# Identity products behind the sums and the transposes of each norm, and another pace for the first layer's modulation

## The chip, the cores and the metric

The kernel runs on one core of a Trainium2 chip. The metric is the device time of one execution in microseconds (us), the median of several executions. The profile is taken of one execution of its own.

## What is computed

Two layers of a transformer trunk over 256 tokens of 2048 values, in float32. Each layer has a mixer and a gated feed-forward part (ffn). Ahead of each stands an RMS norm, scaled and shifted by values that a condition vector `c` gives, and the result is added through a gate of the same kind:

```python
c_act = jax.nn.silu(c)
for i in range(DEPTH):
    mod = c_act @ ada_w[i] + ada_b[i]
    sh1, sc1, g1, sh2, sc2, g2 = [m[:, None, :] for m in jnp.split(mod, 6, axis=-1)]
    h = rms_norm(x, norm_mix_g[i]) * (1.0 + sc1) + sh1
    y = even_mixer(h, ...) if i % 2 == 0 else odd_mixer(h, ...)
    x = x + g1 * y
    h = rms_norm(x, norm_ffn_g[i]) * (1.0 + sc2) + sh2
    x = x + g2 * conv_ffn(h, ffn_w_up[i], ffn_conv_w[i], ffn_conv_b[i], ffn_w_down[i])
return rms_norm(x, final_g)
```

`ada_w[i]` has 2048 rows and 6 x 2048 columns, so the modulation alone reads 192 MiB for both layers.

## The kernel before

**Tiling.** The residual stream `xT` stays in SBUF transposed, as 16 blocks of 128 values by 256 tokens. Weights come in pieces of 128 x 1024 values (512 KB, `make_piece`, L147 to L167) through a ring of six buffers (tile `w`), one piece ahead of use. A piece of the first projection is used as it is, in float32. Every later piece is split: ScalarE rounds it to `hi` (L159), VectorE takes the rest `lo` (L161), and TensorE multiplies three times.

**The modulation.** It has 192 rows (here a row is a 128 x 2048 tile of 1 MB that gives one block of one of the six vectors of a layer). `ada_step` (L109 to L124) starts the transfer of one row on SyncE's queue (SP, L118) into a ring of two buffers (tile `ada`), and VectorE multiplies it by `c_act` and sums it (L120); for a scale one small product more follows (L124). Rows go in the order of use: scale and shift of the first mixer block by block, its gate, scale and shift of the ffn, the ffn's gate, and so on. When a row is asked for is set by a pace: `pacing(rate, ...)` (L131) sets how many rows each weight piece brings, and `beat` (L134) adds the rate at every piece and calls `ada_step` when a whole row is due. Apart from that, `modulate` (L314) asks for a row at once where it needs one. In the opening (L412 to L433) each block of the first norm asks for its two rows so, 32 in all. Then the pace is 0.83 (L434) until the end of `mixer_out`. Between the two stand 26 pieces of the first projection and 32 of the output projection, 58 in all. The first inner norm needs 48 rows beyond the opening's: the gate of the mixer and scale and shift of the ffn. From there the pace is 0.31, later 0.2 and 0.15.

**The norms.** There are five: `in` (opening), then `o0_` ahead of the first ffn, `dn` of layer 0, `o1_`, and `dn` of layer 1 (the last; behind it only the output is scaled and written). `norm_rstd` (L295 to L309) sums the squares over the 128 values of a block on TensorE with a column of ones into tile `nps` (products of one column), VectorE turns the sums into the mean (`v`, L304), GpSimd takes the power -0.5 (`y`, L292), and TensorE transposes it to all partitions (`r`, L308). Then `modulate` makes each block with VectorE and ScalarE.

**What sets the order.** The tile framework's scheduler orders each engine's instructions when the program is built; each engine then works through its list in order. So instructions of the code can change places on an engine, and a changed number moves others. SyncE issues its transfers in order too: behind a row that waits for its buffer the pieces wait.

**The end of the first mixer.** `mixer_out` (L351) multiplies the output projection in two halves of the rows; in each, pairs of blocks are multiplied (`dense2`) and added to `xT` by VectorE (`residual`, L349). In the second half the pairs of blocks also go into the norm's sum (`norm_add`), and the last two blocks are done one by one (`last_blocks`).

Of the kernel before, what the change touches and what calls it, by code (L numbers as in the profile page):

```python
# [60 lines left out]
def trunk(ctx, tc, x, c, params, consts, rel_bias, onehot, w_ada, w_ev, w_o0, w_f0, w_od, w_o1, w_f1, out):  # L61
    nc = tc.nc
# [8 lines left out]
    def bank(tag, name):  # L71
        return ps.tile([P, 512], F32, tag=tag, bufs=BANKS[tag], name=name)
# [19 lines left out]
    def cn(name):  # L92
        a, b = C_AT[name]
        return con[:, a:b]

    ident, exch = cn("ident"), cn("exch")
# [34 lines left out]
    def pacing(rate, hold=0, behind=True):  # L131
        pace.update(rate=rate, hold=hold, behind=behind)
# [106 lines left out]
    def halved(acc):  # L239
        return acc.rearrange("p (j s) -> p j s", j=2)  # L240
# [48 lines left out]
    def rsqrt(v, name):  # L289

        y = work.tile([P, 2], F32, tag="rs_y", bufs=2, name=f"y_{name}")
        nc.gpsimd.tensor_tensor(y, v, mhalf, op=ALU.pow)  # L292
        return y

    def norm_rstd(st):  # L295

        t = bank("t", f"nps_{st['name']}")
        parts = [st["sum"][:, j] for j in range(2)] + st["last"]
        for i, part in enumerate(parts):
            for q in range(2):  # L300
                nc.tensor.matmul(t[:, q:q + 1], part[:, q * P:(q + 1) * P], ones, start=i == 0 and q == 0,
                                 stop=i == len(parts) - 1, skip_group_check=True)
        v = work.tile([P, 2], F32, tag="rs_v", bufs=2, name=f"v_{st['name']}")
        nc.vector.tensor_scalar(v, t[:, :2], 1.0 / D, EPS, op0=ALU.mult, op1=ALU.add)  # L304
        y = rsqrt(v, st["name"])
        r = bank("t", f"r_{st['name']}")
        for q in range(2):
            nc.tensor.transpose(r[:, q * P:(q + 1) * P], y[:, q:q + 1].to_broadcast([P, P]), ident)  # L308
        return r[:, :S]  # L309

    def modulated(name):
# [74 lines left out]
    def even_mixer():  # L386
        with ExitStack() as es:
# [33 lines left out]
            nst = {"name": "in", "sum": total[:, 0:2], "last": [total[:, 2], total[:, 3]]}  # L421
            r = pool.tile([P, 384], F32, tag="z", bufs=2, name="r_in")[:, :S]
            nc.scalar.activation(r, norm_rstd(nst), AF.Copy)
            early = [(token_steps32, bank("acc", "c_lat")), (token_steps32, bank("acc", "va"))]
            early += [(pair_steps32, bank(tag, f"pair{i}")) for i, tag in enumerate(("acc", "s", "s", "o", "t", "t"))]
# [5 lines left out]
                    else:  # L431
                        pair_steps32(acc, hT, [k], 0, DB - 1)
            c_acc, va_acc, p0, p1, p2, p3, p4, p5 = [halved(acc) for _, acc in early]  # L433
            pacing(0.83, 0, False)  # L434
            nc.sync.dma_start(par[:, P_EARLY:], params[:, P_EARLY:])
            nc.sync.dma_start(con[:, P:], consts[:, P:C_W])

# [382 lines left out]


    nst = even_mixer()
    pacing(0.31, 0)
    nst = ffn(norm_rstd(nst), 0)
    pacing(0.2, 5)
    nst = odd_mixer(norm_rstd(nst))
    pacing(0.15, 5)
    nst = ffn(norm_rstd(nst), 1)
# [132 lines left out]
```

## Time and profile before

| | us |
|---|---|
| median of 3 runs | 2358.72 (2341.0 to 2361.32) |
| profiled execution | 2362.08 |
| its span | 2360.3 |

The mean granted clock of TensorE is 0.99 in the profiled execution. A profile counts an engine as busy while an instruction of its runs. "Idle before <-releaser" is the time that an engine stood still ahead of an instruction, and what ended that. The granted clock is a share of TensorE's full clock of 2.4 GHz; 0.50 is its lower level, 1.2 GHz. A float32 product shows as two records.

### The profile page before, as it was taken

What the parts mean: (1) busy time and instruction counts of PE and PEld (TensorE: products, weight loads), DVE (VectorE), ACT (ScalarE), POOL (GpSimd) and SP (SyncE); (2) the same over time, 40 slices, a digit from 0 to 9 for tenths busy, and PEclk for the clock granted to TensorE, in tenths of its full rate; (3) what the DMA queues carried; (4) which work ended last, traced back from release to release, by engine and by line L of the source; (5) the groups of instructions that cost most, each with busy time, mean ns of one, the idle gap of its engine ahead of it and who ended that gap; (6) DMA issues with size and microseconds to landing.
All of it is one profiled execution on the core that took longest, in us unless ns stands there. A gap on an engine that the chain in (4) does not pass through costs nothing.

```text
span 2360.3 us, 44197 instructions
## 1 busy us (share of the span) xinstructions
PE 2283.0 (97%) x18340; PEld 2240.1 (95%) x18340; DVE 1738.4 (74%) x2390; ACT 1092.9 (46%) x1553; POOL 12.0 (1%) x26
## 2 busy tenths in 40 slices
PE   5889999899999999999999999999999999999998
PEld 4768899899999999999999999999999999999998
DVE  4557689998887888888887676878766656656655
ACT  1013354455553554454456655645555445445434
POOL 1000000000000000000000000000000000000000
PEclk9999999999999999999999999999999999999999
DMA  8998988788888888888867777676766666666663
GB/s 313 344 335 326 331 305 312 286 313 302 303 298 299 304 300 304 300 304 301 304 226 240 237 238 239 226 260 204 231 188 187 187 186 185 188 187 187 188 187 118
DMA packets 141929, 606.03 MB, mean 257 GB/s; under 512 B 15584, under 2 KB 20256, under 8 KB 117024
## 3 DMA queue, kind: packets, MB, share of 16 engines
q1 hardware_dynamic: 136656, 597.67, 74.8%
q10 hardware_dynamic: 5072, 5.54, 0.8%
q8 instruction: 143, 2.34, 0.4%
q14 instruction: 58, 0.48, 0.1%
HBM read 601.00 MB, written 2.15 MB: 256 GB/s over the span
## 4 chain that ended last, share of the span: by engine, by line
PE 53%; issue 32%; DMA 7%; DVE 6%; ACT 1%; POOL 0%; ACTq 0%; DVEq 0%; POOLq 0%; SPq 0%
PE up L215 7%; PE up L213 7%; PE up L214 7%; DMA ada<-in_w_ada_dram 6%; DVE ada L120 4%; PE dn L213 3%; PE dn L214 3%; PE dn L215 3%; PE o L213 2%; PE o L215 2%; PE o L214 2%; PE cq L213 1%; PE ck L213 1%; PE cq L214 1%; PE ck L214 1%
## 5 line engine op out<-in xcount | busy, mean ns | idle before, releaser
L159 ACT ACTIVATE hi<-w 128x1024 fp32r<-128x1024 f32 x688 | 728.6, 1059 | 890.7 <-PE up L214 389.6
L161 DVE TENSOR_TENSOR lo<-w,hi 128x1024 fp32r<-128x1024 f32 x688 | 840.5, 1223 | 402.5 <-ACT hi L159 399.9
L213 PE MATMUL up<-hT_f,hi 128*128 128x256 f32 x2816 | 789.5, 281 | 2.8 <-ACT hT_f L323 2.2
L215 PE MATMUL up<-hT_f,lo 128*128 128x256 f32 x2816 | 788.6, 280 | 0.2 <-DVE lo L161 0.2
L214 PE MATMUL up<-hT_f,hi 128*128 128x256 f32 x2816 | 787.4, 280 | 0.0
L213 PEld LDWEIGHTS up<-hT_f,hi 128*128 128x128 f32 x2816 | 529.5, 188 | 3.7 <-ACT hT_f L323 2.9
L215 PEld LDWEIGHTS up<-hT_f,lo 128*128 128x128 f32 x2816 | 530.6, 189 | 0.5 <-DVE lo L161 0.4
L214 PEld LDWEIGHTS up<-hT_f,hi 128*128 128x128 f32 x2816 | 529.9, 188 | 0.0
L120 DVE CUSTOM_DVE_ANT_0 ada<-ada,c_act,par 128x2048 f32<-128x2048 f32 x192 | 450.5, 2346 | 78.8 <-DMA ada<-in_w_ada_dram 78.7
L214 PE MATMUL dn<-gT,hi 128*128 128x256 f32 x1364 | 383.8, 281 | 0.0
L215 PE MATMUL dn<-gT,lo 128*128 128x256 f32 x1364 | 383.8, 281 | 0.0
L213 PE MATMUL dn<-gT,hi 128*128 128x256 f32 x1364 | 383.8, 281 | 0.0
L215 PEld LDWEIGHTS dn<-gT,lo 128*128 128x128 f32 x1364 | 262.1, 192 | 0.0
L213 PEld LDWEIGHTS dn<-gT,hi 128*128 128x128 f32 x1364 | 256.1, 188 | 0.0
L214 PEld LDWEIGHTS dn<-gT,hi 128*128 128x128 f32 x1364 | 256.1, 188 | 0.0
L228 PE MATMUL pair<-hT_m,w 128*128 128x256 f32 x384 | 89.1, 390 | 0.0
L228 PEld LDWEIGHTS pair<-hT_m,w 128*128 128x128 f32 x384 | 76.6, 199 | 11.6
L349 DVE SCALAR_TENSOR_TENSOR xT<-dn,mod,xT 128x256 f32<-128x256 f32 x128 | 56.4, 478 | 25.4 <-PE dn L215 20.2
L228 PE MATMUL q<-hT_m,w 128*128 128x256 f32 x320 | 73.7, 382 | 0.0
L213 PE MATMUL cq<-hT_m,hi 128*128 128x256 f32 x256 | 72.2, 282 | 1.1 <-ACT hT_m L323 1.1
L214 PE MATMUL cq<-hT_m,hi 128*128 128x256 f32 x256 | 72.1, 282 | 0.0
L213 PE MATMUL ck<-hT_m,hi 128*128 128x256 f32 x256 | 72.0, 281 | 0.0
(260 smaller groups left out, 3071.3 us busy)
## 6 DMA issues: line engine op xcount, KB each, us to landing
w<-in_w_f_dram SPq DMA_DIRECT2D x528, 512.0 KB, 4.4
ada<-in_w_ada_dram SPq DMA_DIRECT2D x192, 1024.0 KB, 6.5
w<-in_w_od_dram SPq DMA_DIRECT2D x96, 512.0 KB, 4.4
w<-in_w_o_dram SPq DMA_DIRECT2D x64, 512.0 KB, 5.3
w<-in_w_ev_dram SPq DMA_DIRECT2D x58, 512.0 KB, 7.9
bias<-bias_rows ACTq DMA_DIRECT2D x16, 256.0 KB, 6.2
xT<-in_x_dram SPq DMA_DIRECT2D x4, 512.0 KB, 7.6
c_act<-in_c_dram SPq DMA_DIRECT2D x1, 1024.0 KB, 4.9
```

Source lines behind the costliest of these rows:

```text
L120: nc.vector.tensor_tensor_reduce(w, w, c_act, scale=1.0, scalar=pr("ada_b")[:, s * DB + b:s * DB + b + 1], op0=ALU.mult, op1=ALU.add, accu ...
L159: nc.scalar.activation(hi, raw, AF.Copy)
L161: sub = nc.vector.tensor_tensor(lo, raw, hi.bitcast(F32), op=ALU.subtract)
L213: nc.tensor.matmul(o, hi[:, js], xh, start=k == first and j == 0, stop=False, skip_group_check=True)
L214: nc.tensor.matmul(o, hi[:, js], xl, start=False, stop=False, skip_group_check=True)
L215: nc.tensor.matmul(o, lo[:, js], xh, start=False, stop=k == last, skip_group_check=True)
L228: nc.tensor.matmul(acc[:, j * S:(j + 1) * S], w[:, j * P:(j + 1) * P], xs[:, k], start=k == first and j == 0, stop=k == last, skip_group_c ...
L349: nc.vector.scalar_tensor_tensor(xT[:, b], acc, g, xT[:, b], op0=ALU.mult, op1=ALU.add)
```

## The change

A new helper `busy` multiplies the identity by itself n times, 128 x 128, into columns 128 to 255 of the tile that holds the norm's sums in its first two columns. Nobody reads these columns. `norm_rstd` calls it with 4 behind the products of the sums and with 6 behind the transposes, in all five norms. And the pace of the first layer's modulation behind the opening is 0.95 rows for each piece instead of 0.83.

```diff
--- before.py
+++ after.py
@@ -292,6 +292,11 @@
         nc.gpsimd.tensor_tensor(y, v, mhalf, op=ALU.pow)
         return y
 
+    def busy(spare, n):
+
+        for i in range(n):
+            nc.tensor.matmul(spare, ident, ident, start=False, stop=i == n - 1, skip_group_check=True)
+
     def norm_rstd(st):
 
         t = bank("t", f"nps_{st['name']}")
@@ -300,12 +305,14 @@
             for q in range(2):
                 nc.tensor.matmul(t[:, q:q + 1], part[:, q * P:(q + 1) * P], ones, start=i == 0 and q == 0,
                                  stop=i == len(parts) - 1, skip_group_check=True)
+        busy(t[:, 128:256], 4)
         v = work.tile([P, 2], F32, tag="rs_v", bufs=2, name=f"v_{st['name']}")
         nc.vector.tensor_scalar(v, t[:, :2], 1.0 / D, EPS, op0=ALU.mult, op1=ALU.add)
         y = rsqrt(v, st["name"])
         r = bank("t", f"r_{st['name']}")
         for q in range(2):
             nc.tensor.transpose(r[:, q * P:(q + 1) * P], y[:, q:q + 1].to_broadcast([P, P]), ident)
+        busy(t[:, 128:256], 6)
         return r[:, :S]
 
     def modulated(name):
@@ -431,7 +438,7 @@
                     else:
                         pair_steps32(acc, hT, [k], 0, DB - 1)
             c_acc, va_acc, p0, p1, p2, p3, p4, p5 = [halved(acc) for _, acc in early]
-            pacing(0.83, 0, False)
+            pacing(0.95, 0, False)
             nc.sync.dma_start(par[:, P_EARLY:], params[:, P_EARLY:])
             nc.sync.dma_start(con[:, P:], consts[:, P:C_W])
```

The lists of three engines change as follows. Line numbers of the changed kernel are larger by 5 behind the helper, by 6 behind the first call and by 7 behind the second. Each of the changed lists has the same operations under other buffer numbers.

VectorE at the norm of the opening; `v_in` is the read of the sums, `ada` with the line under it is one row's reduction, `a` its scale, `xn_m` the first block. Before:

```order
L420 TENSOR_TENSOR sq_in_110<-sq_in_110,sq_in_118 128x1024
L304 TENSOR_SCALAR v_in<-nps_in 128x2
L120 ISA ada_147,mod<-ada_147,c_act,par 128x2048
L120 ISA mod 128x1
L124 SCALAR_TENSOR_TENSOR a_93<-mod,par 128x1
L319 SCALAR_TENSOR_TENSOR xn_m_154<-r_in,a_93,xT 128x256
L120 ISA ada_151,mod<-ada_151,c_act,par 128x2048
```

After the change:

```order
L427 TENSOR_TENSOR sq_in_110<-sq_in_110,sq_in_118 128x1024
L120 ISA ada_157,mod<-ada_157,c_act,par 128x2048
L120 ISA mod 128x1
L310 TENSOR_SCALAR v_in<-nps_in 128x2
L124 SCALAR_TENSOR_TENSOR a_93<-mod,par 128x1
L120 ISA ada_161,mod<-ada_161,c_act,par 128x2048
L120 ISA mod 128x1
L326 SCALAR_TENSOR_TENSOR xn_m_164<-r_in,a_93,xT 128x256
L120 ISA ada_189,mod<-ada_189,c_act,par 128x2048
```

The first row's reduction stands ahead of the read of the sums, and the second ahead of the first block.

VectorE ahead of the first inner norm; `xT<-o_1_14` and `xT<-o_1_15` are the last two residuals of the mixer, `v_o` the norm's read, `xn_f` its first block. Before:

```order
L120 ISA mod 128x1
L286 TENSOR_TENSOR nsum_o__2755<-nsum_o__2755,sq_o_12_3112 128x512
L124 SCALAR_TENSOR_TENSOR a_95<-mod,par 128x1
L349 SCALAR_TENSOR_TENSOR xT<-o_1_14_3115,mod,xT 128x256
L161 TENSOR_TENSOR lo_3158<-w_3154,hi_3156 128x1024
L120 ISA ada_3160,mod<-ada_3160,c_act,par 128x2048
L120 ISA mod 128x1
L349 SCALAR_TENSOR_TENSOR xT<-o_1_15_3153,mod,xT 128x256
L161 TENSOR_TENSOR lo_3250<-w_3246,hi_3248 128x1024
L304 TENSOR_SCALAR v_o__3200<-nps_o__3191 128x2
L161 TENSOR_TENSOR lo_3280<-w_3276,hi_3278 128x1024
L319 SCALAR_TENSOR_TENSOR xn_f_3214<-r_o__3204,a_95,xT 128x256
```

After the change:

```order
L356 SCALAR_TENSOR_TENSOR xT<-o_1_14_3147,mod,xT 128x256
L120 ISA ada_3115,mod<-ada_3115,c_act,par 128x2048
L120 ISA mod 128x1
L161 TENSOR_TENSOR lo_3152<-w_3148,hi_3150 128x1024
L120 ISA ada_3154,mod<-ada_3154,c_act,par 128x2048
L120 ISA mod 128x1
L356 SCALAR_TENSOR_TENSOR xT<-o_1_15_3184,mod,xT 128x256
L161 TENSOR_TENSOR lo_3189<-w_3185,hi_3187 128x1024
L310 TENSOR_SCALAR v_o__3235<-nps_o__3222 128x2
L120 ISA ada_3191,mod<-ada_3191,c_act,par 128x2048
L120 ISA mod 128x1
L326 SCALAR_TENSOR_TENSOR xn_f_3255<-r_o__3239,a_95,xT 128x256
```

Ahead of the last residual stand two rows with one split between them instead of one row, and directly behind the norm's read stands a row where a split stood. Over a longer stretch, from the second residual of pair 4 of the second half (`o_1_4`) to the norm's read, VectorE's list has 6 rows before and 10 now; from the start of the program to that read it has 80 before and 86 now. The 192nd row ends 64 splits earlier.

TensorE at the same norm; `nps_o` are its sums, `r_o` the transposes, `up` the first products of the ffn. Before:

```order
L192 MATMUL o_1_15_3153<-oT_o__1706,hi_3118 128x256
L193 MATMUL o_1_15_3153<-oT_o__1706,lo_3120 128x256
L301 MATMUL nps_o__3191<-ones,nsum_o__2755 128x1 x4
L301 MATMUL nps_o__3191<-ones,sql_o_14_3151 128x1 x2
L301 MATMUL nps_o__3191<-ones,sql_o_15_3188 128x1 x2
L308 MATMUL r_o__3204<-con,y_o__3202 128x128 x2
L213 MATMUL up_0_3211<-hT_f_3210,hi_3156 128x256
L213 MATMUL up_1_3212<-hT_f_3210,hi_3248 128x256
```

After the change:

```order
L192 MATMUL o_1_15_3184<-oT_o__1726,hi_3150 128x256
L193 MATMUL o_1_15_3184<-oT_o__1726,lo_3152 128x256
L306 MATMUL nps_o__3222<-ones,sql_o_15_3219 128x1 x2
L298 MATMUL nps_o__3222<-con 128x128 x5
L314 MATMUL r_o__3239<-con,y_o__3237 128x128 x2
L298 MATMUL nps_o__3222<-con 128x128 x5
L213 MATMUL up_0_3252<-hT_f_3251,hi_3187 128x256
L213 MATMUL up_1_3253<-hT_f_3251,hi_3289 128x256
```

Of the sums only those of block 15 (`sql_o_15`) still stand directly ahead of the read; those of the pairs and of block 14 have moved ahead of the 24 products of block 15. Of the ten identity products (L298) five stand ahead of the transposes and five behind them. The read of the sums (`v_o`) waits for the fourth of the first five, the fifth waits for that read.

## Rows read from the trace of the kernel before

**Rows 1.** part 1 of the page: busy us of each engine (share of the span), instructions.

```profile
PE 2283.0 (97%) x18340; PEld 2240.1 (95%) x18340; DVE 1738.4 (74%) x2390; ACT 1092.9 (46%) x1553; POOL 12.0 (1%) x26
```

**Rows 2.** stretches: us, engines' busy us (instructions), granted clock, DMA share, GB/s.

```profile
30.00:170.00 140.00, 118.00 (x480) 97.86 (x480) 79.26 (x90) 7.42 (x15) 0.00 (x0) 0.94 0.92 338
170.00:330.00 160.00, 155.44 (x895) 139.39 (x896) 113.70 (x285) 70.07 (x203) 0.73 (x1) 1.00 0.90 328
330.00:398.00 68.00, 67.88 (x569) 66.89 (x569) 62.88 (x120) 34.79 (x78) 0.00 (x0) 1.00 0.85 302
398.00:444.00 46.00, 39.62 (x324) 38.65 (x323) 44.60 (x59) 19.44 (x23) 0.00 (x0) 0.97 0.89 331
```

**Rows 3.** chain of waits from 405 to 445 us: shares by line, one piece.

```profile
by line: DVE ada L120 34.1%; DMA ada<-in_w_ada_dram 16.0%; DVE lo L161 15.4%; DVE xT L349 9.9%; DVE nsum_o__2755 L286 6.4%; issue 4.4%; POOL y_o__3202 L292 3.8%; PE nps_o__3191 L301 2.6%; PE o L215 2.4%; PE o L213 2.4%; PE o L214 2.3%; ACT 
...
428.73 6.41 DMA ada<-in_w_ada_dram
```

**Rows 4.** VectorE's timeline: start, us, engine, line, operation, count, [idle before <-releaser].

```profile
409.97 0.87 DVE L349 SCALAR_TENSOR_TENSOR xT<-o,mod,xT 128x256 f32<-128x256 f32 x2
...
435.16 2.35 DVE L120 CUSTOM_DVE_ANT_0 ada<-ada,c_act,par 128x2048 f32<-128x2048 f32 x1 [0.46 <-DMA ada<-in_w_ada_dram]
...
439.63 2.35 DVE L120 CUSTOM_DVE_ANT_0 ada<-ada,c_act,par 128x2048 f32<-128x2048 f32 x1
...
441.90 0.48 DVE L349 SCALAR_TENSOR_TENSOR xT<-o,mod,xT 128x256 f32<-128x256 f32 x1
...
443.94 0.16 DVE L304 TENSOR_SCALAR v_o__3200<-nps_o__3191 128x2 f32<-128x2 f32 x1 [0.42 <-PE nps_o__3191 L301]
```

**Rows 5.** TensorE's timeline at that norm, same columns.

```profile
442.89 1.01 PE L301 MATMUL nps_o__3191<-ones,sql_o 128*128 128x1 f32 x4 [3.15 <-ACT sql_o L275]
...
447.66 1.01 PE L213 MATMUL up<-hT_f,hi 128*128 128x256 f32 x3 [1.12 <-ACT hT_f L323]
```

**Rows 6.** busy time and granted clock by stretch, columns as in Rows 2.

```profile
448.00:451.00 3.00, 3.00 (x15) 3.00 (x15) 3.00 (x9) 1.71 (x5) 0.00 (x0) 0.50 0.98 412
1199.00:1200.00 1.00, 0.20 (x2) 0.12 (x2) 0.56 (x2) 0.00 (x0) 0.35 (x1) 0.68 0.74 295
1202.00:1206.00 4.00, 3.79 (x18) 3.80 (x18) 4.00 (x11) 2.26 (x6) 0.00 (x0) 0.50 0.12 46
```

**Rows 7.** timeline of all engines in the opening.

```profile
22.84 0.16 DVE L304 TENSOR_SCALAR v_in<-nps_in 128x2 f32<-128x2 f32 x1 [3.67 <-PE nps_in L301]
...
25.29 4.83 SPq L118 DMA_DIRECT2D ada<-in_w_ada_dram  x2
...
27.41 2.35 DVE L120 CUSTOM_DVE_ANT_0 ada<-ada,c_act,par 128x2048 f32<-128x2048 f32 x1
```

**Rows 8.** busy time of the opening's norm, columns as in Rows 2.

```profile
22.00:26.00 4.00, 0.93 (x5) 0.85 (x6) 2.59 (x4) 0.00 (x0) 2.74 (x1) 1.00 0.00 0
```

**Rows 9.** GpSimd's power (L292): count, ns min/median/max, first and last start.

```profile
L292 POOL TENSOR_TENSOR y_dn<-v_dn,mhalf x2: 688/692/696, 1199.6 to 2349.1; 128x2 f32<-128x2 f32 x2
L292 POOL TENSOR_TENSOR y_in<-v_in,mhalf x1: 2739/2739/2739, 23.1 to 23.1; 128x2 f32<-128x2 f32 x1
...
L292 POOL TENSOR_TENSOR y_o__3202<-v_o__3200,mhalf x1: 1544/1544/1544, 444.3 to 444.3; 128x2 f32<-128x2 f32 x1
```

**Rows 10.** TensorE's timeline, 0 to 60 us.

```profile
19.22 3.58 PE L301 MATMUL nps_in<-ones,sq_in 128*128 128x1 f32 x16 [10.76 <-DVE sq_in L420]
...
41.58 5.34 PE L228 MATMUL pair<-hT_m,w 128*128 128x256 f32 x24
46.76 1.03 PE L221 MATMUL c_lat<-w,hT_m 128*128 128x256 f32 x4
```

**Rows 11.** timeline of all engines at the dn norm of layer 0.

```profile
1198.60 0.61 PE L301 MATMUL nps_dn<-ones,sql_dn 128*128 128x1 f32 x4 [0.15 <-ACT sql_dn L275]
1199.41 0.15 DVE L304 TENSOR_SCALAR v_dn<-nps_dn 128x2 f32<-128x2 f32 x1
```

**Rows 12.** modulation rows (tile ada) from 300 to 444 us.

```profile
DMA to landing us min/median/max: 4.8/6.6/8.6
```

## The prediction

> **What bounds the kernel now.** I read the page first: TensorE's rows fill 97% of the span [rows 1]. So only the places where it waits can change the end. The busy time by stage shows where they are [rows 2]. From 170 to 398 us TensorE is full or nearly so. From 398 to 444 us it is busy 39.6 us of 46 and VectorE 44.6 of 46: there VectorE sets the pace. Next the chain of waits for the end of that stretch: VectorE's reductions of modulation rows (L120) are 34.1% of the chain from 405 to 445 us, and the transfer of a row another 16.0% [rows 3]. The reader is to see in the longest piece that a row's weights were issued at 428.73 us and landed 6.41 us later, with VectorE waiting. VectorE's timeline shows what is late: the last residual before the norm stands behind a row of 2.35 us and ends only after 442 us [rows 4]. TensorE waited 3.15 us for the square made from it, and 1.12 us more for the first modulated block [rows 5].
>
> The clock of that norm is 0.50 behind it (448 to 451 us: 15 products in 3 us, the lower level, 1.2 GHz) [rows 6]. The full stretch before, at clock 1.00 (2.4 GHz), ran 569 products in 67.9 us, 0.119 each [rows 2]. At the norm after the first layer's ffn (dn) the clock falls within the microsecond from 1199 (0.68, so at about 1199.4) and is 0.50 to 1206 us; 18 products take 3.79 us there [rows 6], 0.21 each. So the lower level costs 18 x (0.21 - 0.119) = 1.7 us a norm. The opening, 30 to 170 us, is ruled by the modulation rows' transfers (DMA share 0.92, clock 0.94 [rows 2]).
>
> **The change, part by part.** *A: the opening.* The identity products put off the norm's read of the sums, and the build therefore sets the first row's reduction ahead of it. VectorE was idle 3.67 us before 22.84 us [rows 7], so the reduction now runs from about 19.2 to 21.5 us. It frees the row's buffer then instead of at 25.3 us, when SP issued the third row [rows 7]. The DMA engines moved nothing from 22 to 26 us [rows 8], so they are free to take it. The second row's reduction can run behind the norm's read. That read comes 1.8 us later (below): 24.6 us, reduction to 27.0 instead of 29.7 us (27.41 + 2.35 [rows 7]). After that each block's odd row waits for a buffer freed by the odd row before it, so the shift travels through the opening: 2.7 us by the odd rows, 1.3 by the even (the first block's product, after the Pool's 2.74 us [rows 9], moves by nothing). I take -2.3; bounds 0 (a later transfer eats it) and -3.8 (25.3 - 21.5).
>
> *B: the pace.* From the opening to the first norm 58 pieces are issued: 0.83 x 58 = 48 rows, exactly those that the norm needs; 0.95 x 58 = 55, seven rows of the next gate as well. By the order, at the norm's read VectorE has reduced 80 rows in the kernel before, 86 now. Two of the six stand before 330 us, where VectorE is busy 114 of 160 us [rows 2]: hidden there. Without that cover they would cost 4.5. Four stand after the second residual of pair 4 of the last half (410.4 us), where 6 rows become 10. That is the stretch where VectorE is the chain. A row holds VectorE 2.27 us (439.63 to 441.90 [rows 4]): 4 x 2.27 = 9.1 us, less 0.9 us in which VectorE stood idle before 435.16 and 443.94 [rows 4]. The rows now also come in twos, and two buffers hold them. A row's transfer can be issued only when the row two before it is reduced, so two rows take at least 6.4 + 2.3 = 8.7 us [rows 3], ten 43.5; VectorE's work from 410.4 us to the read is 34 + 9 = 43. Nearly equal, and unevenly spread: I add half a transfer, 3.2 us, and take B = +12 rounded. Lower bound 0 (all six in idle time; a gain is excluded, since in both orders a row still stands right before the last residual). Upper bound: all six at half of transfer plus reduction, 6 x (6.41 + 2.27) / 2 = +26. SP issues in order, so the pieces behind a waiting row wait with it; that is inside these bounds. The sums of block 14 now stand ahead of block 15's 24 products on TensorE; these take 2.8 us and lie beside the last row's reduction and its transfer. The rows saved later (seven at the end of the pacing) bring nothing, as TensorE is full there.
>
> *C: the fill.* The four products ahead of the read lengthen each norm, because the read waits for the last of them (one tile). An fp32 product is two records. At the upper level 24 records of 256 columns take 5.2 us (41.58 to 46.76 [rows 10]), 0.108 us for 128 columns, so four products are 0.86 us. At the lower level even one column takes 3.58 / 16 = 0.224 us a record [rows 10]: 1.8 us. The fifth runs while the Pool works. The five after the transposes take 1.07 or 2.2 us, in a gap of 1.12 us [rows 5]: nothing, or +1.0.
> First norm: TensorE stood idle before it, so the lower level: +1.7 (four products), +1.0 (five), minus half of the 1.7 us that an earlier rise could give. Then the Pool: its power took 0.69 us with VectorE idle, 1.54 beside a split of 1.23 us, 2.74 beside a row of 2.35 us [rows 9]. It ends as VectorE's instruction does. Now a row stands right behind the read instead of a split: +1.2. The Trainium skill (SBUF — State Buffer, "SBUF: two separate sides") says that VectorE and GpSimd share a port pair held for a whole instruction. The three rows agree with it. By that rule alone the same 2.74 us would be expected, and the sum is unchanged. First norm together: +3.0 (bounds +0.3 and +3.9).
> Second and third of the inner norms: +0.65 each for the four products (at dn the sums were ready at 1199.21 us and the read began at 1199.41, behind a split [rows 11]: 0.2 us are hidden). If the clock stays up, -1.7: -1.05 each. If it falls, +1.0 more: +1.7 each at most. The clock fell at about 1199.4 us [rows 6], just behind the sums' last products, one column each, which ended at 1199.21 [rows 11], and the fill starts just there: I take the middle, 0. Last norm: nothing follows on TensorE, its read is put off by 0.86: +0.9 (bound +1.8).
>
> Sum: -2.3 + 12 + 3.0 + 0 + 0.9 = +13.6 us on the profiled execution's 2362.1, 2375.7. Its span of 2360.3 has 1.8 us around it. That execution lies 3.4 us above the median, 2358.7; I forecast the median: 2358.7 + 13.6 = 2372.
>
> **The rivals.** *R1, the extra rows are hidden.* VectorE has 5 us idle from 330 to 398 us [rows 2], and rows started earlier could be done earlier. For it: VectorE alone is not the chain before 398. Against: the order puts ten rows where six stood. With B = 0 and the clock kept in all norms: -2.3 + 0.3 - 2.1 + 0.9 = -3, 2355.
> *R2, the fill does nothing for the clock.* The clock falls at the end of the sums' products whatever follows them. Then +3.9 at the first norm, +1.7 at two more: -2.3 + 12 + 3.9 + 3.4 + 0.9 = +18, 2377.
> *R3, the two buffers bind the whole stage (slower).* From 300 to 444 us rows took 4.8 to 8.6 us to land, in the middle 6.6 [rows 12]. Now 31 rows fall into those 144 us; each takes half of landing plus reduction, so the buffers bind from a landing of 144 x 2 / 31 - 2.35 = 6.9 us on. For it: the DMA share is 0.85 to 0.90 [rows 2] and seven more MB come. Against: rows landed sooner than 6.9 us so far. At 8.6 us throughout, 31 x 5.5 = 170: B = +26, sum +28, 2386. One per cent of the time is 23.6 us; this passes it from a landing of about 8.3 us.
> *R4, the fill keeps the clock up everywhere it can.* The rows show the clock still up while the sums' products ran [rows 6, 11]. With -1.05 at two norms and +0.3 at the first: -2.3 + 12 + 0.3 - 2.1 + 0.9 = +9, 2367. The Trainium skill (TensorE: Matmul & The Clock Gate, Part 1, "What's actually happening") says the clock is throttled by default and activity releases it; by that rule products that nobody reads count like any others, which would give this case.
>
> **How the numbers follow.** My forecast 0.38 (2372), R4 0.20 (2367), R1 0.17 (2355), R2 0.12 (2377), R3 0.10 (2386 and above), 0.03 for a gain of over 1% that no row shows. The range leaves out about 0.1 on the slow side and less on the other. The three times of the kernel before spread from 2341 to 2361 with nothing changed, and the low end makes room for a part of that: 2350 to 2385. A measurement of this kernel can tell about 1% (23.6 us) from no change. Faster by that: 0.03. Slower: R3 and a tail, 0.10. The rest, 0.87, is within it.
>
> **What would show it.** A: the first L120 reduction starts near 19.2 us, and the opening's last block comes 2 to 3 us earlier. B: in the 46 us before the first norm's read VectorE's rows (L120) hold more time, VectorE waits for row transfers, and the read (443.94 us before) comes 8 to 13 us later, TensorE idle that much longer. If it comes at or before 444 us, B is wrong and R1 holds. C: the Pool's power at the first norm takes 2.7 us; the granted clock after the two inner norms tells R4 from R2; the last norm's read comes 0.9 us later behind the last dense product. If rows take over 7 us to land from 300 us on, R3 is at work.

## The result and the profile after

The changed kernel takes 2366.64 us (median of 20 runs, 2348.41 to 2377.53), the kernel before 2351.85 us (median of 20 runs, 2338.57 to 2361.32). The ratio is 1.0055 with a 95% interval of 1.0036 to 1.0074: about 13 us slower, 8.5 to 17.4. The forecast was 2372 within 2350 to 2385, by +13.6 us on the kernel before. The time lies in the range, and the size of the change is near the forecast's. The forecast stood on the median of three runs, 2358.72; that of the twenty is 2351.85, so the time came out 5 us lower than forecast while the change was forecast well.

The profiled execution of the changed kernel took only 2349.73 us, 12 us **less** than the profiled one of before. So the two traces can't be compared by their spans. What can be compared are stages: from one mark of the program to the next, as read from the starts of instructions. The marks are the read of the opening's norm (`v_in`), the first product `q` behind the opening, the first product `o` of the output projection, and the reads of the four later norms (o0, dn of layer 0, o1, last). A second profile of each kernel (e4 and e7 below) shows how far a stage wanders by itself:

| stage, us | before | e4, before again | after | e7, after again |
|---|---|---|---|---|
| start to `v_in` | 22.8 | 23.0 | 25.0 | 24.8 |
| `v_in` to `q` (opening) | 154.8 | 154.1 | 146.2 | 144.1 |
| `q` to `o` | 139.1 | 137.3 | 135.9 | 136.2 |
| `o` to read of o0 | 127.2 | 127.0 | 138.0 | 137.8 |
| read of o0 to read of dn | 755.5 | 755.6 | 760.2 | 760.1 |
| dn to o1 | 397.4 | 396.8 | 396.7 | 396.6 |
| o1 to last | 752.1 | 753.6 | 735.7 | 752.1 |
| last to end | 11.4 | 11.2 | 10.3 | 10.5 |

The three stages from `o` to the read of o1 come back within about 0.5 us for the same kernel. Two stages are the changed kernel's loss, by the means of the two profiles: +10.8 us from `o` to the first inner norm, +4.6 us from there to the next. From `q` to `o` it gains 2.2. The opening and the last ffn differ between executions by more than the change does, and the last ffn of one kernel ran in 735.7 and in 752.1 us.

Busy time of the changed kernel by stretch, the same stretches and columns as [rows 2], and then the last 8 us of the third in two parts:

```profile
170.00:330.00 160.00, 158.46 (x945) 143.03 (x944) 123.75 (x306) 70.98 (x208) 0.00 (x0) 1.00 0.93 337
330.00:398.00 68.00, 67.53 (x569) 66.82 (x568) 65.91 (x112) 34.21 (x67) 0.00 (x0) 1.00 0.88 318
398.00:444.00 46.00, 35.05 (x250) 33.15 (x250) 41.91 (x48) 12.20 (x15) 0.00 (x0) 0.89 0.88 331
436.00:440.00 4.00, 2.65 (x12) 2.65 (x13) 3.61 (x5) 0.99 (x1) 0.00 (x0) 0.50 0.79 295
440.00:444.00 4.00, 2.98 (x17) 2.68 (x16) 1.59 (x4) 0.49 (x2) 0.00 (x0) 0.65 1.00 395
```

In the 46 us that end at 444 TensorE has 250 instructions where it had 324 [rows 2], and its granted clock is 0.89 instead of 0.97. VectorE is busy 65.9 of 68 us already before 398 us.

VectorE's timeline of the changed kernel ahead of the norm, as in [rows 4]:

```profile
429.52 2.35 DVE L120 CUSTOM_DVE_ANT_0 ada<-ada,c_act,par 128x2048 f32<-128x2048 f32 x1 [0.19 <-DMA ada<-in_w_ada_dram]
...
437.69 2.35 DVE L120 CUSTOM_DVE_ANT_0 ada<-ada,c_act,par 128x2048 f32<-128x2048 f32 x1 [0.39 <-DMA ada<-in_w_ada_dram]
...
442.46 0.48 DVE L356 SCALAR_TENSOR_TENSOR xT<-o,mod,xT 128x256 f32<-128x256 f32 x1 [2.41 <-PE o L193]
...
445.09 0.16 DVE L310 TENSOR_SCALAR v_o__3235<-nps_o__3222 128x2 f32<-128x2 f32 x1 [1.01 <-PE nps_o__3222 L298]
445.21 2.35 DVE L120 CUSTOM_DVE_ANT_0 ada<-ada,c_act,par 128x2048 f32<-128x2048 f32 x1
```

The last residual (442.46) waits 2.41 us for TensorE in this profile. TensorE's timeline there shows why, as in [rows 5]:

```profile
428.99 0.46 PE L193 MATMUL o<-oT_o__1726,lo 128*128 128x256 f32 x1 [2.71 <-DVE lo L161]
...
437.36 0.58 PE L193 MATMUL o<-oT_o__1726,lo 128*128 128x256 f32 x1 [1.50 <-DVE lo L161]
...
443.91 1.14 PE L298 MATMUL nps_o__3222<-con 128*128 128x128 f32 x8
445.30 0.49 PE L298 MATMUL nps_o__3222<-con 128*128 128x128 f32 x2 [0.25 <-DVE v_o__3235 L310]
448.16 0.69 PE L314 MATMUL r_o__3239<-con,y_o__3237 128*128 128x128 f32 x2 [2.37 <-POOL y_o__3237 L292]
448.64 2.34 PE L298 MATMUL nps_o__3222<-con 128*128 128x128 f32 x10
...
464.54 0.39 PE L213 MATMUL up<-hT_f,hi 128*128 128x256 f32 x1 [0.79 <-ACT hi L159]
465.75 0.39 PE L215 MATMUL up<-hT_f,lo 128*128 128x256 f32 x1 [0.70 <-DVE lo L161]
```

After its waits for splits the clock is 0.50 (436 to 440 us above), and the last 22 of block 15's 24 products run from 437.4 to 442.4 us: 5 us, where 24 products take 2.8 at clock 1.00 (0.118 each). The fill's four products ahead of the read and five behind the transposes are the L298 rows.

### The profile page after: what moved, and what is told of

Same layout as the page of the kernel before. It is cut to its first block, busy times and chain, and to the rows that moved or that the text cites. A ratio compares the mean times of both kernels' runs of the same rounds, so it can differ in the third digit from the quotient of the medians.

```text
span 2347.9 us, 44418 instructions
## 1 busy us (share of the span) xinstructions
PE 2279.1 (97%) x18440; PEld 2236.7 (95%) x18440; DVE 1740.4 (74%) x2390; ACT 1093.8 (47%) x1553; POOL 13.3 (1%) x26
## 4 chain that ended last, share of the span: by engine, by line
PE 54%; issue 32%; DVE 6%; DMA 5%; ACT 1%; POOL 0%; DVEq 0%; POOLq 0%; ACTq 0%
PE up L215 7%; PE up L213 7%; PE up L214 7%; DMA ada<-in_w_ada_dram 5%; PE dn L213 3%; PE dn L215 3%; PE dn L214 3%; DVE ada L120 3%; PE q L228 2%; PE o L215 2%; PE o L213 2%; PE o L214 2%; PE ck L213 1%; PE ck L214 1%; PE cq L214 1%
## 5 line engine op out<-in xcount | busy, mean ns | idle before, releaser
L120 DVE CUSTOM_DVE_ANT_0 ada<-ada,c_act,par 128x2048 f32<-128x2048 f32 x192 | 450.3, 2346 | 68.2 <-DMA ada<-in_w_ada_dram 68.1
L213 PE MATMUL ck<-hT_m,hi 128*128 128x256 f32 x256 | 71.8, 281 | 0.0
L215 PE MATMUL o<-oT_o__1726,lo 128*128 128x256 f32 x240 | 67.2, 281 | 4.6 <-DVE lo L161 4.6
L214 PE MATMUL ck<-hT_m,hi 128*128 128x256 f32 x256 | 71.6, 280 | 0.0
```

What stands on the lines that cost most here:

```text
L120: nc.vector.tensor_tensor_reduce(w, w, c_act, scale=1.0, scalar=pr("ada_b")[:, s * DB + b:s * DB + b + 1], op0=ALU.mult, op1=ALU.add, accu ...
L213: nc.tensor.matmul(o, hi[:, js], xh, start=k == first and j == 0, stop=False, skip_group_check=True)
L214: nc.tensor.matmul(o, hi[:, js], xl, start=False, stop=False, skip_group_check=True)
L215: nc.tensor.matmul(o, lo[:, js], xh, start=False, stop=k == last, skip_group_check=True)
```

## Experiments

All stages below are from `o` to the first inner norm's read unless another is named. The kernel before is timed beside each.

**e1, the pace alone, and e2, the fill alone.**

```diff
e1, on before:
-            pacing(0.83, 0, False)
+            pacing(0.95, 0, False)
e2, on after:
-            pacing(0.95, 0, False)
+            pacing(0.83, 0, False)
```

> Only the pace is 0.95; no identity products. VectorE's list has 86 rows ahead of the first inner norm, as in the changed kernel. Theory (the six rows that the faster pace adds ahead of that norm cost the time): +12 us on the median of before, 2364; TensorE idle in the 46 us before the norm about as much as in the changed kernel (11 us against 6 before). Rival (the fill costs the time: the reads wait for it, and the order changes around it): 0 +- 2 us, 2352. Second rival (both take a part): +6, 2358.

> Only the identity products; the pace stays 0.83 and VectorE's list has 80 rows ahead of the first inner norm, as before. Theory (pace costs the time): opening -2.3, first norm +2 (no row behind its read, so the power stays near 1.5 us), two inner norms -1.05 each since the profile of the changed kernel shows the clock at 1.00 there, last norm +0.9: sum -1.5 us, 2350. Rival (fill costs the time): +12, 2364.

e1: 2363.42 us against 2354.39, ratio 1.0035 (1.0001 to 1.0069), +8 us. e2: 2346.88 us, ratio 0.9973 (0.9941 to 1.0006), between 14 us faster and 1 us slower. The pace costs the time; the fill alone costs none that can be measured. Singly the two come to +2 us (8 - 6), together to +13. The intervals of the two single runs are just wide enough for such a difference, so their times don't settle whether the parts add up; by stages a part of some 3 us comes only with both (below, C). The stage in before, e1 and e2, each from its own trace (columns as in [rows 2]):

```profile
316.70:443.90 127.20, 120.75 (x995) 118.26 (x995) 119.97 (x213) 64.23 (x130) 0.00 (x0) 0.99 0.86 310
```

```profile
301.80:438.70 136.90, 125.57 (x995) 121.89 (x995) 129.82 (x222) 62.11 (x129) 0.00 (x0) 0.96 0.89 324
```

```profile
301.90:430.40 128.50, 122.63 (x1003) 119.94 (x1003) 121.09 (x215) 64.30 (x130) 0.00 (x0) 0.98 0.86 310
```

The pace alone makes the stage 9.7 us longer with the same 995 TensorE instructions. Half of it is idle time (127.20 - 120.75 = 6.5 us before, 136.90 - 125.57 = 11.3 now), the other half is TensorE's own busy time, 120.75 to 125.57, at a mean granted clock of 0.96: behind the waits the clock is 0.50 (406 to 409 us and 430 to 436 us), and products then run slower. In before 22 rows start in the stage, with the pace 26 (and one runs when it begins): 2.4 us a row. The fill adds 1.3 us.

**e3, the pace 0.95, but no row beyond the 80 that the norm needs.** `beat` stops at 80 rows until the next `pacing`; no fill.

```diff
+            if ada["made"] < pace["cap"]:
                 ada_step()
...
-            pacing(0.83, 0, False)
+            pacing(0.95, 0, False, 80)
```

> The pace is 0.95 without the fill, but stops once the 80 rows that the first inner norm needs are asked for, and goes on behind the norm. The six early rows of the gate are then not ahead of the norm; the last row ahead of it stands three pairs of blocks earlier than before. Theory (the rows right before the norm cost the time, not the faster pace as such): TensorE's waits of 6 us in the last 16 us before the norm shrink to 1 to 3 us, some 3 us of waits come at the pairs where rows now stand: -1 to -4 us on before, 2349. Rival (a faster pace costs wherever its rows stand, through the DMA engines and the two buffers): +6 to +12, 2358 to 2364.

2348.34 us, ratio 0.9976 (0.9952 to 1.0001). The loss is gone. But the stage did not become shorter, as the theory had it: 128.3 us, in which 20 rows start, against 127.1 with 22. The waits had only moved to an earlier place: TensorE waits 0.91, 1.55, 0.61 and 1.47 us between 405 and 419 us, where the rows now crowd, and 0.15 us instead of 3.15 right at the norm.

**e4 and e7, second profiles** of the kernel before and of the changed one; their stages stand in the table above.

> The kernel before, unchanged, for a second profile. It shows how far two executions of one kernel differ by stage. If the layer-1 ffn's 752 us (read of its norm to the last norm's read) are a property of the kernel, they return within 2 us, and the 736 us of the changed kernel come from the change; if they differ from execution to execution, a product spacing between 0.113 and 0.118 us shows up here too. The opening's end (177.6 us) should return within 3 us if it is the kernel's, and wander by 5 us or more if it is set by the DMA rate of the execution.

> The changed kernel, unchanged, for a second profile. The stage from the output projection's first product to the norm's read should return at 138 +- 1 us and that from there to the next norm's read at 760 +- 1 us if both belong to the kernel (127.1 and 755.6 before); the opening and the layer-1 ffn may differ by 10 us or more from the first profile, as they did between executions of kernels that have the same instructions there.

Both as the first profiles for the stages that carry the change. For e4 the opening and the last ffn came back too, for e7 the last ffn did not (752.1 instead of 735.7).

**e5, e6 and e9: half a row's sum, half its transfer, both.** All on e1, for the ten rows 76 to 85 only, one profile each; these kernels leave out a part of ten modulation values.

```diff
+        n = D // 2 if 76 <= i < 86 else D
...
e6, e9:
-        nc.sync.dma_start(w, w_ada[i])
+        nc.sync.dma_start(w[:, :n], w_ada[i][:, :n])
e5, e9 (e6 does the same line D // n times):
-        nc.vector.tensor_tensor_reduce(w, w, c_act, ...)
+        nc.vector.tensor_tensor_reduce(w[:, :n], w[:, :n], c_act[:, :n], ...)
```

> The pace is 0.95 without the fill; the ten rows 76 to 85, those that stand in the last stretch ahead of the first inner norm, are summed over their first 1024 columns only (the transfer stays whole; so these ten modulation values leave half of their sum out). VectorE spends some 1.2 us less on each; the order of rows ahead of the norm is nearly the same. Measured by the stage from the first product of the output projection to the norm's read, 136.9 us with the pace alone and 127.1 before. Theory (VectorE's time is the chain): 125 to 128 us. Rival (the transfer into one of two buffers is the chain: half of 6.4 + 1.2 instead of half of 6.4 + 2.35 for each of ten rows): 131 to 134 us.

> The pace is 0.95 without the fill; the same ten rows transfer only their first 1024 columns (0.5 MB) and VectorE sums these twice, so that its time for a row stays (2 x 1.25 us) and the transfer is halved; ten modulation values hold twice the half sum instead of the sum. The build sets one more whole row ahead of the norm (87). Same stage. Theory (VectorE's time is the chain): 136 to 140 us, nothing gained. Rival (the transfers are the chain): 127 to 131 us. In between: each has its share.

> The pace is 0.95 without the fill; the ten rows 76 to 85 transfer only their first 1024 columns and are summed over these only (ten modulation values leave half of their sum out). Stage from the output projection's first product to the norm's read: 136.9 us with the pace alone; 137.4 with half the sum alone, 140.9 with half the transfer alone. Theory A (two limits that are nearly equal, VectorE's row time and the row's transfer into two buffers; taking one away leaves the other): 124 to 128 us. Theory B (neither: the weight pieces that stand behind rows on SP's queue come late whatever a row costs): 134 to 138 us.

e5: 137.4 us. The theory that VectorE's time alone is the chain falls, and the rival's 131 to 134 is missed too. VectorE's busy time fell by 10 us, and nothing was gained:

```profile
309.80:447.20 137.40, 124.27 (x997) 120.67 (x996) 119.88 (x222) 62.15 (x129) 0.00 (x0) 0.96 0.89 326
```

e6: 140.9 us with the transfers halved. That is just above where the theory put it (136 to 140), but it holds one whole row more and 0.2 us more for each split sum:

```profile
311.30:452.20 140.90, 126.07 (x995) 121.88 (x995) 134.35 (x244) 64.24 (x131) 0.00 (x0) 0.97 0.85 299
```

What replaces VectorE in e5 is a weight piece behind two rows. SP's own timeline of e5 (when it issued which transfer), and TensorE's wait for that piece:

```profile
408.97 2.79 SPq L118 DMA_DIRECT2D ada<-in_w_ada_dram  x2
412.16 0.33 SPq L154 DMA_DIRECT2D w<-in_w_o_dram  x1
```

```profile
422.96 0.58 PE L215 MATMUL o<-oT_o__1716,hi 128*128 128x256 f32 x1 [6.36 <-ACT hi L161]
```

The second row of the pair waited for its buffer, the piece behind it went out at 412.16 us, into the same DMA engines as 2 MB of rows, and TensorE stood 6.36 us for its `hi`. So in this trace, with half the sums, the rows' transfers and the queue behind them bind; with half the transfers VectorE does. This one wait is half of e5's idle time of 13.1 us, and no second trace tells whether it comes back. With both halved (e9) the stage falls to 131.4 us, though VectorE's list has one row more ahead of the norm than in e1:

```profile
313.80:445.20 131.40, 122.45 (x995) 118.52 (x995) 123.37 (x223) 63.96 (x131) 0.00 (x0) 1.00 0.88 312
```

That is between theory A's 124 to 128 and B's 134 to 138. Two limits of nearly equal size would explain that one alone brings nothing; three single traces fit that and don't prove it. They don't account for all of it: 9 us of TensorE idle time are left, 5 of them waits for a split on VectorE, and how much of these the build's other order of rows makes is open.

**e8, fill, and the 80 rows even earlier: pace 1.15 with e3's stop at 80.**

```diff
-            pacing(0.95, 0, False)
+            pacing(1.15, 0, False, 80)
```

> Fill as in the changed kernel, pace 1.15 that stops at the 80 rows of the first inner norm: VectorE has all 80 behind it at the end of the first half of the output projection, and the second half holds none but one of the gate. Theory (rows right ahead of the norm cost, rows in the stretch where VectorE is 70% busy don't): the stage to the norm's read falls from 127 to 121 to 124 us, the stage ahead of it grows by 0 to 2 us: 2346, -6 us on before. Rival (the DMA engines, 0.90 busy in that stretch, bring weights late): the stages ahead of it grow by 5 to 10 us, 2355 to 2360.

2367.03 us, ratio 1.0066 (1.0042 to 1.0089): 15 us slower, the rival's side and beyond. All but three of the 80 rows were done before the second half of the output projection (from 394.8 us; the last ended at 406.4), and it still lost. `q` to `o` took 140.6 us, `o` to the read 131.7 with 20 rows only. TensorE's timeline in the first half of the output projection shows where the waits went:

```profile
374.17 0.39 PE L216 MATMUL o<-oT_o__1744,lo 128*128 128x256 f32 x1 [1.60 <-DVE lo L162]
...
382.51 0.38 PE L216 MATMUL o<-oT_o__1744,lo 128*128 128x256 f32 x1 [1.72 <-DVE lo L162]
...
390.85 0.58 PE L216 MATMUL o<-oT_o__1744,lo 128*128 128x256 f32 x1 [2.63 <-DVE lo L162]
```

VectorE is late with `lo` here as well. So it is not the place right ahead of the norm that costs but rows that come too close in the output projection. A piece there gives TensorE 24 products, 24 x 0.118 = 2.8 us. VectorE has a split of 1.22 us for it, and 0.83 rows of 2.35 us are 1.95 more: 3.2 us, above 2.8, before any residual. With 0.95 it is 3.45, with 1.15 3.9. (A count that takes in the rest of VectorE's work stands at e12.) In the first projection a piece has no split. The forecast of 2346 failed because it took the first half of the output projection for a stretch with spare VectorE time.

**e10, rows on GpSimd's queue (from row 32 on), pace 0.95, no fill.**

```diff
-        nc.sync.dma_start(w, w_ada[i])
+        dma = nc.sync if i < 32 else nc.gpsimd
+        dma.dma_start(w, w_ada[i])
```

> The pace is 0.95 without the fill; from row 32 on (behind the opening) GpSimd's queue issues the modulation rows instead of SP's, so that a row that waits for its buffer no longer holds up the weight pieces behind it. All rows are whole; the build sets 87 rows ahead of the norm. Same stage. Theory A (two buffers and VectorE): 134 to 139 us, since rows take as long as before. Theory B (the in-order queue delays the pieces): 128 to 132 us, and TensorE's waits for hi and lo shrink.

2375.1 us (one run). The stage took 122.0 us, below both theories. But the stage ahead of it grew from 136.6 to 168.6 us, with 34 rows in it instead of 28, and in this one 20 start (e1: 26):

```profile
176.00:344.60 168.60, 147.30 (x758) 128.82 (x756) 116.89 (x262) 56.70 (x166) 18.25 (x34) 0.93 0.89 320
344.60:466.60 122.00, 119.93 (x995) 117.80 (x995) 117.61 (x208) 64.18 (x130) 11.13 (x21) 1.00 0.89 322
```

The build set seven more rows ahead of the output projection, so this run doesn't tell whether the in-order queue or the number of rows freed the stage. It shows that 20 evenly spread rows leave TensorE 2 us of idle time in it, at a clock of 1.00. The longer stage ahead fits the two buffers: its rows landed 7.4 us after their issue in the median, and 34 x (7.4 + 2.35) / 2 = 166 us, an estimate; VectorE waited 45.3 us for rows there, 13.0 in e1. Each row issue kept GpSimd busy for 0.53 us (11.13 us for 21).

**e11, on the changed kernel: only the six products behind the transposes, and the pace back at 0.83** (one profile).

```diff
-        busy(t[:, 128:256], 4)
...
-            pacing(0.95, 0, False)
+            pacing(0.83, 0, False)
```

> Pace 0.83; only the six identity products behind the transposes, none ahead of the read of the sums. Read at the two inner norms whose clock the whole fill kept up (dn of layer 0, o1): if the products ahead of the read are what keeps it up, the granted clock falls to 0.50 there for 3 us or more, as without fill, and 0 to 1.7 us a norm are lost again; if those behind the transposes do, the clock stays at 1.00 and the four ahead only cost: the stage from norm to norm is then 0.4 to 0.9 us shorter than with the whole fill. In the opening the read comes at 22.8 us again and the first row's sum stands behind it: third row issued near 25.3 us instead of 21.6.

The clock at the inner norms, 10 us each around dn and o1: first the changed kernel's second profile (e7), then e11, then the fill alone (e2, 10 and 13 us):

```profile
1200.00:1210.00 10.00, 9.31 (x73) 8.55 (x73) 7.65 (x19) 4.33 (x9) 1.25 (x3) 1.00 0.31 109
1598.00:1608.00 10.00, 9.38 (x73) 8.60 (x74) 7.66 (x18) 4.45 (x10) 0.69 (x1) 1.00 0.25 88
```

```profile
1197.00:1207.00 10.00, 9.14 (x63) 8.78 (x62) 8.02 (x19) 3.98 (x8) 1.26 (x3) 0.83 0.37 113
1594.00:1604.00 10.00, 9.43 (x67) 8.99 (x66) 7.77 (x18) 4.47 (x9) 0.70 (x1) 0.83 0.42 159
```

```profile
1184.00:1194.00 10.00, 9.30 (x63) 8.84 (x63) 7.33 (x17) 3.15 (x8) 0.70 (x1) 0.83 0.26 96
1581.00:1594.00 13.00, 12.53 (x79) 11.88 (x80) 8.06 (x19) 5.20 (x11) 0.69 (x1) 0.74 0.31 109
```

The opening's read came at 22.8 us again, as expected. Without the four ahead of the read the clock falls at both inner norms, as expected of the first alternative. But with the whole fill it stays up in both profiles of the changed kernel and falls in that of e2, which runs the same products at these norms. The two other profiles with the whole fill differ as well: in e8 it falls at both norms (0.83 over 10 us from 1190, 0.66 from 1588 us), in e12 it stays at 1.00 at dn (from 1187 us) and falls at o1 (0.83 from 1583 us). So the fill alone does not decide it, and what else does is open. The price is small either way: dn to o1 takes 396.6 and 396.7 us in the changed kernel, 397.0 in e11, 398.4 in e2, 398.9 in e8, 396.1 in e12, 396.8 and 397.4 before.

**e12, fill, and two paces:** 1.08 rows for each of the 26 pieces of the first projection, 0.63 for each of the 32 of the output projection.

```diff
-            pacing(0.95, 0, False)
+            pacing(1.08, 0, False)
...
+            pacing(0.63, 0, False)
             return mixer_out(oS, 0, steps, "o0_", 2)
```

> The whole fill; the pace is 1.08 rows for each of the 26 pieces of the first projection and 0.63 for each of the 32 of the output projection, 48 rows together as with 0.83. VectorE's list has 80 rows ahead of the norm, evenly spread; 20 of them fall in the stage from the output projection's first product to the norm's read, 22 before, 27 with the pace of 0.95. Theory (the time of that stage follows the rows in it, 9.8 us for 5 rows, 2.0 each): 127.1 - 4 = 123 us for the stage, the one ahead of it as before, so 2345 to 2349, -4 us on before and as much on the fill alone within what a measurement tells. Rival (the pace in the first projection costs, as with 1.15 and the cap, where that stage took 140.6 us and the next 131.7): 2356 or more.

2341.49 us against 2353.01, ratio 0.9961 (0.9937 to 0.9985): 9 us faster than before, 4 to 15. With 0.63 the split and the rows of a piece are 1.22 + 1.48 = 2.7 us on VectorE, below TensorE's 2.8, and the stage loses nearly all of its idle time:

```profile
313.20:434.80 121.60, 120.38 (x1003) 118.61 (x1003) 115.19 (x209) 64.38 (x130) 0.00 (x0) 1.00 0.90 331
```

121.6 us, below the 123 expected; `q` to `o` took 140.6, 2.4 us above the mean of before. The interval overlaps that of the fill alone, so what the two paces add to the fill is shown by the stage, not by the time.

The sum of 2.7 us leaves out VectorE's residuals and the norm's sums; with a residual of 0.43 us a piece (0.87 for two, [rows 4]) even 0.63 would be above 2.8. Where the rows really fall settles it. In the stage's first eight pieces TensorE also has the mixer's remaining steps to do, and eight or nine rows start there in before, e1 and e12. From the ninth piece on it has only the 24 products of each piece, 24 x 2.8 = 68 us for 24 pieces. From there to the norm's read, all engines and below that VectorE's rows alone (busy us, count), in before, e1 and e12:

```profile
366.30:443.90 77.60, 71.31 (x594) 70.35 (x592) 73.31 (x93) 31.88 (x38) 0.00 (x0) 0.99 0.90 331
366.30:443.90 77.60, 31.42 (x14) 0.99 0.90 331
```

```profile
351.70:438.70 87.00, 76.29 (x598) 74.23 (x596) 83.03 (x102) 30.48 (x36) 0.00 (x0) 0.94 0.90 333
351.70:438.70 87.00, 42.10 (x18) 0.94 0.90 333
```

```profile
363.10:434.80 71.70, 70.81 (x602) 70.53 (x600) 68.82 (x87) 32.26 (x38) 0.00 (x0) 1.00 0.92 339
363.10:434.80 71.70, 25.80 (x11) 1.00 0.92 339
```

VectorE's other work there is 41 to 43 us each time (73.31 - 31.42, 83.03 - 42.10, 68.82 - 25.80). Beside 68 us of products that leaves room for some 11 rows of 2.35 us, and e12 has 11, before 14, e1 18. Rows that come close together cost more than their number: e8 has 11 there too and takes 82.6 us.

## Why the prediction was right

**A, the opening.** The order worked as forecast. Timeline of the changed kernel, all engines, as in [rows 7]:

```profile
19.32 2.35 DVE L120 CUSTOM_DVE_ANT_0 ada<-ada,c_act,par 128x2048 f32<-128x2048 f32 x1
...
21.70 0.33 SPq L118 DMA_DIRECT2D ada<-in_w_ada_dram  x1
...
24.98 0.16 DVE L310 TENSOR_SCALAR v_in<-nps_in 128x2 f32<-128x2 f32 x1 [3.31 <-PE nps_in L298]
```

The reduction starts at 19.3 us (forecast 19.2), the third row is issued at 21.7 (21.5), the read comes at 24.98 (24.6). The -2.3 us that should follow can't be read from one trace: with the same instructions in the opening, it ended at 177.6 us in before and at 165.2 in e1. Over all profiles, `q` starts at 175.0 us on average in the nine whose norm has no products ahead of the read (165.2 to 178.3) and at 169.9 in the five that have them (163.7 to 173.3). The sign agrees, the size is not settled.

**B, the pace.** Forecast +12, bounds 0 and +26. e1 puts it at +9.7 us in the stage and +1.3 in the next (756.9 against 755.6), with `q` to `o` 1.6 us shorter: +9.4, and +8 by the time. The place and the size were right, the size in part by luck. Two steps of its working were not right. *VectorE's time of 9.1 us as the cause:* VectorE's busy time in the stage did grow by 9.9 us (119.97 to 129.82), and TensorE's waits are for splits that VectorE makes late. But halving ten rows' sums brought nothing (e5): in that trace the transfers into two buffers and a piece behind them bound at the same level. The prediction had called the two "nearly equal" (43.5 and 43 us) and added half a transfer; e5, e6 and e9, one trace each, agree with that. *The products of block 15 "lie beside the last row's reduction":* not all of them do. The waits let the clock fall, and these products took 5 us. The last residual waited 2.41 us for them in the first profile, 0.42 in e7 and 1.00 in e1; as the stage is equally long in both profiles of the changed kernel, this wait does not set its length. The clock's part in the stage, half of the 9.7 us, was priced nowhere. That the sum came out right nevertheless is luck: the longer chain through VectorE had been priced in its stead.

**C, the fill.** First norm: forecast +3.0, bounds +0.3 and +3.9. Against the pace alone, the changed kernel takes 1.1 us more up to the read (138.0 to 136.9) and 3.3 more behind it (760.2 to 756.9): +4.4, above the bound. The four products were priced at the lower level by [rows 10]; but the profile gives that stretch (19.2 to 22.8 us) a clock of 1.00, so that row does not show the level. The runs show the price: the eight records took 2.05 us in e2, at 0.50, and 1.14 us in the changed kernel, where the clock was at 1.00 again (forecast 1.8 and 0.86). The Pool's step was right: with a row right behind the read its power takes 2.71 us, forecast 2.74. In e1 and e2, where no row and no split runs beside it, it takes 0.69, as in the undisturbed norms of before [rows 9]. The rule of the Trainium skill that the prediction named (SBUF — State Buffer, "SBUF: two separate sides") agrees with these rows. First the changed kernel, then e2:

```profile
L292 POOL TENSOR_TENSOR y_o__3237<-v_o__3235,mhalf x1: 2712/2712/2712, 445.4 to 445.4; 128x2 f32<-128x2 f32 x1
```

```profile
L292 POOL TENSOR_TENSOR y_o__3216<-v_o__3214,mhalf x1: 691/691/691, 430.7 to 430.7; 128x2 f32<-128x2 f32 x1
```

So the fill by itself costs 1.3 us there (e2). With the pace alone (e1) no row stands directly behind the read either; it stands there only in the build that has both, and the price is then 4.4. What the sum left out is the wait after the norm: `hi` and `lo` come 0.79 and 0.70 us late at 464.5 and 465.8 us, and the clock is 0.77 from 464 to 469 us; in before `hi` came 0.61 us late there, `lo` in time, and the clock was 1.00 (461 to 467 us).

Inner norms: forecast 0 between -1.05 and +1.7 each; dn to o1 went from 397.1 to 396.6, -0.5. The clock stayed up (rival R4's condition) in both profiles of the changed kernel, but not in e2 and e8, so R4 is neither shown nor excluded as a rule; the Trainium skill's sentence that activity releases the clock (TensorE: Matmul & The Clock Gate, Part 1, "What's actually happening") fits the changed kernel's profiles and does not tell why those two differ. Last norm: +0.9 forecast; from its read to the end nothing grew (11.3 to 10.4), and what its four products cost ahead of the read is lost in a stage that varies by 16 us.

**The rivals.** R1 (extra rows hidden) is excluded by e1. R2's condition held in e2 and e8, not in the changed kernel. R3's first half, that the two buffers bind, is what e5 shows; its second half, landings above 8 us throughout, did not come: rows of the changed kernel landed in 5.8 us in the median from 300 to 444 us (6.3 in e7).

**A test that was wrong.** The prediction said that a read at or before 444 us would prove B wrong. It came at 445.1 and, in the second profile, at 442.9 us, because the opening had ended 6 to 9 us earlier in these executions. By that test R1 would have won in the second profile, while the stage itself had grown by 11 us. A time from the start of the program adds up every stage ahead of it, and here one of them wanders by more than the effect.

## What to carry to other kernels

Where rows of side work are spread over a stage by a rate, compare the side engine's whole work with the main engine's, in the stretch where the main engine has least to do for each unit. Here that is the output projection's last 24 pieces: 42 us of other work on VectorE and 2.35 us a row against 68 us on TensorE, room for some 11 rows. The rate of 0.63 put 11 there, 0.83 put 14 and 0.95 put 18. More of it earlier helps only as far as the stage ahead has the room: the first projection has no splits, but 34 rows ahead of the output projection (e10) made that stage 168.6 us long. And test such a change on a stage between two marks, in two profiles of each kernel, not on clock time from the start.

## What the runs showed of the hardware

*Two spacings of the same products at the same granted clock.* In the last ffn of the changed kernel 40 us held 355 products in one execution and 342 in the other, both at clock 1.00 (first the first profile, then e7):

```profile
1640.00:1680.00 40.00, 40.00 (x355) 40.00 (x354) 30.48 (x46) 23.60 (x35) 0.00 (x0) 1.00 0.64 190
```

```profile
1640.00:1680.00 40.00, 40.00 (x342) 40.00 (x341) 28.96 (x45) 22.12 (x32) 0.00 (x0) 1.00 0.62 187
```

That is 0.113 against 0.117 us a product, and it comes in stretches of 20 to 200 us. The last ffn is 736 to 754 us long, in kernels with the same instructions there, and together with the opening (142 to 156 us without products ahead of its read) that is enough for the spread of the 20 runs. Its cause is open.

*Waits cost twice.* In the stage of e1 the added idle time of 4.9 us came with 4.8 us of slower products: behind the waits the granted clock was 0.50, from 406 to 409 and from 430 to 436 us.
